# One encoder layer on one core: the first projections split the next block's weights during this block's products, without GpSimd

## The chip, the core and the metric

The kernel runs on one core of a Trainium2 chip. The core has five engines that each run their own instruction queue in order: TensorE (PE in the rows; its weight loads are PEld), VectorE (DVE), ScalarE (ACT), GpSimd (POOL) and SyncE (SP), which here only issues transfers. An engine waits at an instruction until the instructions or transfers of others that it depends on are done. The metric is the device time of one execution in microseconds (us). Time before: 1261.2 us, the median of three runs (1259.64 to 1262.53).

## The reference

One encoder layer over 512 tokens of width 1024, in float32. Only the head of it matters here: a conditioning vector gives six modulation vectors, the first two of which scale and shift x, and the result u is projected by one wide matrix.

```python
mod = jnp.einsum('bd,dn->bn', silu(c), w_ada) + b_ada           # 1024 -> 6 * 1024
sh_a, sc_a, g_a, sh_f, sc_f, g_f = jnp.split(mod[:, None, :], 6, axis=-1)
u = x * (1.0 + sc_a) + sh_a
proj = jnp.einsum('bsd,dn->bsn', u, w_in)                       # 512 x 1024 by 1024 x 1952
cq, ckv, k_rope, dq, dk, dv = jnp.split(proj, IN_SPLITS, axis=-1)
...                                                             # latent attention and differential attention
s12 = einsum('bqhmd,bkhmd->bmhqk', dqb, dk) * DIFF_SCALE + bias # bias from the relative positions
p12 = softmax(s12);  a = p12[:, 0] - lam * p12[:, 1]
...                                                             # output projection, layer norm
ffn = expert_choice_ffn(u, w_router, w_gate, w_up, w_down)      # 16 experts, 64 tokens each
```

## The kernel before

All large operands stand in 24 pages of the on-chip memory, each 128 partitions by 8 KB; `pages.get` and `pages.put` hand out whole pages or parts of them while the program is built, and a transfer or a write into a reused page waits for its last reader.

**Stage 1** (the loop `for i in range(KB)`, L409 to L455) runs over the eight blocks i of 128 input features. For each block four transfers come in on SP's queue, two blocks ahead (`stage1_load`): two of 512 KB with rows of w_ada (`wadaT`), 256 KB of x transposed (`xt`) and 512 KB of the projection's weights (`wd`, 128 by 1024). Then:

- `mod_finish` on VectorE: two multiply-and-sum passes over 128 by 1024 (L217), each with a read of its accumulator, and two one-column operations (L226, L228) give the block's scale and shift in `modc`.
- ScalarE applies them to `xt` (L416). ScalarE also makes the high part of `xt` and of both halves of `wd` (`hi_of`, L136: a copy rounded to a shorter float), and the low part is the difference to it: of `xt` on VectorE (`split`, L236), of the weights on GpSimd for blocks 1 to 7 and on VectorE for block 0 (L422).
- TensorE multiplies: `mm3` is three products, high by high, high by low, low by high. Four banks take the 512 columns of queries and keys with the weights as the stationary operand, four the 512 columns of values with u as the stationary one: 8 times 3 = 24 products of 128 by 512 a block (L121), 192 in the stage, summed over the blocks in the eight banks. The first product of a block needs the high parts, the second the low part of `xt`, the third the low part of the weights.

In block 0 two small products with `rb` and two copies (L145) prepare the relative-position table, which a transfer `f_d` and a transfer `bias_d<-f_d` (1792 KB) spread out in memory; `bias_steps` (L273, one GpSimd operation) and `bias_table` (L279 to L285) find out whether the positions are consecutive, and a branch on GpSimd skips the general table.

All of this stage's order is written out by hand (`manual_schedule`): each engine runs what stands in the code in that order. The stage ends with `q_split(0)`, `q_split(1)` and `rope_tables`. From `start.close()` on, through both attentions, a planner of the framework sets the order on each engine, from its own estimate of when each operation could start; it is free to move products of the remaining projection columns (`q_mm`, 24 products for each of seven column groups) between the score products (`diff_scores`, L521, 16 units of six products) and the softmax passes (`diff_soft`, L536, which read the score banks and the rows of the bias table loaded at L505). From the layer norm on the order is written by hand again, and the program ends with the 16 experts, whose 403 MB of weights come through SP's queue (`prefetch`, L968) as pages come free.

Of the kernel before, what the change touches and what calls it, by code (L numbers as in the profile page):

```python
# [9 lines left out]
F32R = mybir.dt.float32r  # L10
# [3 lines left out]
OP = mybir.AluOpType  # L14
# [87 lines left out]
def encoder_layer(ctx: ExitStack, tc: tile.TileContext, xT, x, wadaT, cvec, colp, rowp, rows, cst, pos, posr,  # L102
# [28 lines left out]
    def ff(ap):  # L131
        return ap.bitcast(F32)

    def hi_of(eng, dst, src, scale=1.0):
        if eng is ACT:
            return ACT.activation(dst, src, AF.Copy, scale=scale)  # L136
        else:
            assert scale == 1.0
            eng.tensor_copy(dst, src)
# [104 lines left out]
    def stage1_load(i):  # L244
        mw = mod_pair(i, i, 8 + i, True)
        hx, xt = pages.get(2, old=OLD1)
        hw, wd = pages.get(4, old=OLD1)
        if i == 0:
            SP.dma_start(wd[:, :512], w_a[i][:, :512])
            SP.dma_start(xt, xT[i])  # L250
            SP.dma_start(wd[:, 512:], w_a[i][:, 512:])
        else:
            SP.dma_start(xt, xT[i])
            EP["s1"] = SP.dma_start(wd, w_a[i])
        if i == 0:
            SP.dma_start(rb, relb)
            SP.dma_start(ohp[:32], bass.AP(tensor=cst.tensor, offset=cst.offset + C_OH, ap=[[C_W, 32], [1, 1024]]))
        st1[i] = (mw, hx, xt, hw, wd)
# [146 lines left out]
    bias_flag()  # L405
    stage1_load(0)
    stage1_load(1)
    for i in range(KB):
        mw, hx, xt, hw, wd = st1[i]  # L409
        if i != 1:  # L410
            mod_finish(mw)
        whh, pg = pages.get(8, F32R)
        wh = HL(pg[:, :1024], pg[:, 1024:])
        if i == 0:
            hi_of(ACT, wh.hi[:, :512], wd[:, :512])
        ACT.activation(xt, xt, AF.Identity, scale=modc[:, 8 + i:9 + i], bias=modc[:, i:i + 1])  # L416
        uh, u = split(xt, 512, DVE)
        for c in (slice(0, 512), slice(512, 1024)):
            eng = POOL if i else DVE
            if i or c.start:  # L420
                EP["hi"] = hi_of(ACT, wh.hi[:, c], wd[:, c])
            eng.tensor_tensor(wh.lo[:, c], wd[:, c], ff(wh.hi[:, c]), op=OP.subtract)  # L422
        U.append(u)
        Uh.append(uh)
        XT.append(xt)
# [1 line left out]
        pages.put(hw)  # L427
        if i + 2 < KB:
            stage1_load(i + 2)
        for n in range(4):  # L430
            mm3(BK[n], wh[:, n * P:(n + 1) * P], u[:, :], i == 0, i == KB - 1)
        if i == 0:
# [1167 lines left out]
```

## Time and profile before

| | |
|---|---|
| median of three runs | 1261.2 us |
| profiled execution: its time, its span | 1258.0 us, 1256.2 us |
| stage 1, first to last of its 192 products | 11.9 to about 69.6 us |
| busy share of the span: TensorE, VectorE, ScalarE, GpSimd | 93%, 30%, 18%, 5% |
| mean transfer rate over the span, and in the experts' part | 363 GB/s, 421 GB/s |

The time line of the profile gives the start of a piece, its length, the engine, line, tiles and the count of instructions that run without a break, and in brackets the idle time before it with what ended it. The table of waits sums these. A table by stretch gives the busy time of each engine in it, with the granted clock of TensorE (1.00 is 2.4 GHz, 0.50 is 1.2 GHz) and the share of the transfer engines. Engines with a q (SPq) are the engine's issuing queue.

### The profile page before, as it was taken

Reading aid. Unit: us, or ns where it says so; the run is one execution under the profiler, and the core shown is the slowest. Engines: PE = TensorE matmul, PEld = TensorE weight load, DVE = VectorE, ACT = ScalarE, POOL = GpSimd, SP = SyncE. Lnnn points to the kernel's source line nnn. Section 1 sums busy time; section 2 is a strip of 40 time slices with the busy share of each in tenths; the row PEclk is TensorE's granted clock in tenths of the full one; section 3 lists DMA queues with packets and bytes.
Section 4 is the critical chain, followed back from the end, with each engine's and each line's share of the span. In section 5 each row is a group of like instructions: output and inputs, shape, how many; then the busy total and the mean of one; then the engine's idle time right before and its main releaser. Section 6 shows DMA issues by size and latency. Waiting matters only on the chain.

```text
span 1256.2 us, 14042 instructions
## 1 busy us (share of the span) xinstructions
PE 1167.8 (93%) x5657; PEld 553.8 (44%) x5657; DVE 374.9 (30%) x813; ACT 229.4 (18%) x473; POOL 57.1 (5%) x45
## 2 busy tenths in 40 slices
PE   8899998998999999999998799789978997999896
PEld 5677676766434433433433243224323432343232
DVE  5779899867101111010110102010101110111016
ACT  3465785443010000000000000000000000001001
POOL 2500000000000320000000000000000000000003
PEclk8999999999999999999999999999999999999999
DMA  9872524497999999999999999999999999999993
GB/s 341 301 244 86 185 98 167 158 365 284 373 421 421 422 418 421 421 421 421 421 421 421 422 420 422 422 422 421 421 421 421 421 422 421 421 422 421 421 401 149
DMA packets 76360, 456.03 MB, mean 363 GB/s; under 512 B 8285, under 2 KB 8669, under 8 KB 28163
## 3 DMA queue, kind: packets, MB, share of 16 engines
q1 hardware_dynamic: 76002, 455.02, 89.3%
q8 instruction: 44, 0.72, 0.2%
q14 instruction: 24, 0.19, 0.0%
q10 hardware_dynamic: 290, 0.10, 0.0%
HBM read 452.98 MB, written 3.95 MB: 364 GB/s over the span
## 4 chain that ended last, share of the span: by engine, by line
PE 38%; DMA 35%; DVE 2%; issue 0%; POOL 0%; ACT 0%; POOLq 0%; SPq 0%; DVEq 0%; ACTq 0%
PE bk L121 21%; PE bk L1338 16%; DMA pg<-in_w_up_dram 16%; DMA pg<-in_w_gate_dram 9%; DMA pg<-in_w_down_dram 9%; PE bk L1369 1%; DVE small L1212 0%; DVE ohg L1214 0%; POOL pg L1467 0%; DVE lst L1449 0%; PE bk L1262 0%; POOLq L1596 0%; PE bk L1287 0%; DVE mv L1450 0%; DVE pg L1406 0%
## 5 line engine op out<-in xcount | busy, mean ns | idle before, releaser
L1338 PE MATMUL bk<-pg,xs 128*64 128x512 f32 x2048 | 474.3, 601 | 50.5 <-DMA pg<-in_w_up_dram 50.5
L121 PE MATMUL bk<-pg,pg 128*64 128x512 f32 (+3 forms) x2138 | 463.9, 479 | 17.4 <-ACT pg L136 6.0
L121 PEld LDWEIGHTS bk<-pg,pg 128*64 128x64 f32 (+1 forms) x2138 | 236.6, 159 | 195.2 <-issue 130.4
L1338 PEld LDWEIGHTS bk<-pg,xs 128*64 128x64 f32 x2048 | 148.2, 137 | 348.0 <-issue 244.3
L1363 DVE TENSOR_TENSOR pg<-pg,bk 128x512 f32<-128x512 f32 x32 | 21.9, 687 | 341.6 <-PE bk L1338 313.2
L143 ACT ACTIVATE pg<-bk 128x512 f32<-128x512 f32 (+1 forms) x97 | 54.8, 582 | 358.3 <-PE bk L1369 321.3
L1273 DVE TENSOR_TENSOR pg<-pg,bk 128x512 f32<-128x512 f32 x56 | 38.5, 687 | 123.1 <-PE bk L121 122.7
L1256 DVE TENSOR_SCALAR xs<-bk,Gc,Bc 128x128 f32<-128x128 f32 x32 | 13.1, 409 | 206.7 <-PE bk L121 206.7
L121 PEld LDWEIGHTS bk<-ohg,pg 128*128 128x128 f32 x512 | 59.7, 192 | 27.3 <-issue 27.3
L121 PE MATMUL bk<-ohg,pg 128*128 128x128 f32 x512 | 66.1, 282 | 0.5 <-DVE ohg L1244 0.5
L121 PE MATMUL bk<-pg,ohg 128*128 128x512 f32 x120 | 59.3, 617 | 0.2 <-DVE pg L1406 0.2
L1254 ACT ACTIVATE xs<-bk,Bc,Gc 128x128 f32<-128x128 f32 x32 | 14.6, 457 | 199.8 <-PE bk L121 199.8
L143 ACT ACTIVATE ohg<-bk 128x512 f32<-128x512 f32 x8 | 4.8, 597 | 238.1 <-PE bk L1262 238.1
L136 ACT ACTIVATE pg<-pg 128x512 fp32r<-128x512 f32 (+2 forms) x63 | 42.7, 709 | 20.1 <-DVE pg L910 4.0
L236 DVE TENSOR_TENSOR pg<-pg,pg 128x512 fp32r<-128x512 f32 (+1 forms) x40 | 37.1, 936 | 16.5 <-ACT pg L136 16.3
L1423 POOL TENSOR_TENSOR pg<-pg,pg 128x512 f32<-128x512 f32 x4 | 5.1, 1277 | 786.5 <-DVE lst L1422 786.5
L1022 DVE CUSTOM_DVE_ANT_0 pg<-pg,pg 128x1024 f32<-128x1024 f32 x32 | 38.8, 1218 | 1.5 <-DMA pg<-in_wadaT_dram 1.5
L121 PEld LDWEIGHTS bk<-pg,ohg 128*128 128x128 f32 x120 | 20.4, 189 | 38.2 <-issue 37.5
L1406 DVE SCALAR_TENSOR_TENSOR pg<-bk,lst,pg 128x512 f32<-128x512 f32 x16 | 12.0, 751 | 74.2 <-PE bk L121 73.4
L1359 ACT ACTIVATE pg<-bk 128x512 f32<-128x512 f32 x32 | 18.8, 598 | 60.2 <-PE bk L1338 60.2
L1369 PEld LDWEIGHTS bk<-csb,pg 128*128 128x128 f32 x128 | 17.7, 207 | 26.9 <-DVE pg L1363 13.9
L217 DVE CUSTOM_DVE_ANT_0 pg<-pg,pg 128x1024 f32<-128x1024 f32 x16 | 24.6, 1571 | 5.8 <-DMA pg<-in_wadaT_dram 5.8
(223 smaller groups left out, 606.7 us busy)
## 6 DMA issues: line engine op xcount, KB each, us to landing
pg<-in_w_gate_dram SPq DMA_DIRECT2D x128, 1024.0 KB, 19.8
pg<-in_w_up_dram SPq DMA_DIRECT2D x128, 1024.0 KB, 19.8
pg<-in_w_down_dram SPq DMA_DIRECT2D x120, 1024.0 KB, 19.8
pg<-in_wadaT_dram SPq DMA_DIRECT2D x16, 1024.0 KB, 5.0
pg<-in_wadaT_dram SPq DMA_DIRECT2D x16, 512.0 KB, 8.0
pg<-in_w_down_dram SPq DMA_DIRECT2D x16, 512.0 KB, 10.9
pg<-bias_d SPq DMA_DIRECT2D x16, 256.0 KB, 3.5
pg<-in_w_out_dram SPq DMA_DIRECT2D x8, 512.0 KB, 3.2
```

Source lines behind the costliest of these rows:

```text
L121: PE.matmul(o, l, r, start=start, stop=stop)
L136: return ACT.activation(dst, src, AF.Copy, scale=scale)
L143: ACT.activation(dst, src, AF.Copy)
L217: DVE.tensor_tensor_reduce(out=w2[:, j], in0=w2[:, j], in1=cs, scale=1.0, scalar=0.0, op0=OP.mult, op1=OP.add, accum_out=modr[:, n:n + 1])
L236: lo_eng.tensor_tensor(lo, src, ff(hi), op=OP.subtract)
L1022: i = DVE.tensor_tensor_reduce(out=w2[:, j], in0=w2[:, j], in1=cs, scale=1.0, scalar=0.0, op0=OP.mult, op1=OP.add, accum_out=modr[:, n:n + 1])
L1254: ACT.activation(xs[:, k, :], src, AF.Identity, scale=Gc[:, k:k + 1], bias=Bc[:, k:k + 1])
L1273: DVE.tensor_add(acc[t][:, c], acc[t][:, c], bank)
L1338: PE.matmul(banks[c][r], xs[:, k, r], w[e][:, c * 512:(c + 1) * 512], start=k == 0, stop=k == 7)
L1359: ACT.activation(EP["HS"][:, c * 512:(c + 1) * 512], banks[c], AF.Silu)
L1363: DVE.tensor_tensor(s, s, U[c], op=OP.mult)
L1369: PE.transpose(G[c % 2][:, i * P:(i + 1) * P], sj[:, i // 2, i % 2, :], ident)
```

## The change

The loop body is reordered. The page of the split weights of block i+1 is taken, both its high parts are made (`w_hi` on ScalarE) and its modulation rows are summed (`mod_finish` on VectorE) in block i's turn, after block i's own splits and before block i's products in the code, for i from 1 to 6; block 1's modulation rows were summed in block 0's turn already. In turn i VectorE makes the two low parts of the weights (`w_lo`, L419) while ScalarE scales and rounds `xt`, and then the low part of `xt` (L443). All low parts are VectorE's; GpSimd keeps `bias_steps`, two memsets, the flag with its branch, and `rope_tables`. No operation is added or left out, and the transfers and their sizes are the same. Lines after the loop stand 27 lower (L521 is L548 then).

```diff
@@ -405,21 +405,43 @@
     bias_flag()
     stage1_load(0)
     stage1_load(1)
+    HALVES = (slice(0, 512), slice(512, 1024))
+    wsp = {}
+
+    def w_page(i):
+        whh, pg = pages.get(8, F32R)
+        wsp[i] = whh, HL(pg[:, :1024], pg[:, 1024:])
+
+    def w_hi(i, c):
+        EP["hi"] = hi_of(ACT, wsp[i][1].hi[:, c], st1[i][4][:, c])
+
+    def w_lo(i, c):
+        DVE.tensor_tensor(wsp[i][1].lo[:, c], st1[i][4][:, c], ff(wsp[i][1].hi[:, c]), op=OP.subtract)
+
+
     for i in range(KB):
         mw, hx, xt, hw, wd = st1[i]
-        if i != 1:
+        if i == 0:
             mod_finish(mw)
-        whh, pg = pages.get(8, F32R)
-        wh = HL(pg[:, :1024], pg[:, 1024:])
+        if i < 2:
+            w_page(i)
         if i == 0:
-            hi_of(ACT, wh.hi[:, :512], wd[:, :512])
+            w_hi(0, HALVES[0])
         ACT.activation(xt, xt, AF.Identity, scale=modc[:, 8 + i:9 + i], bias=modc[:, i:i + 1])
-        uh, u = split(xt, 512, DVE)
-        for c in (slice(0, 512), slice(512, 1024)):
-            eng = POOL if i else DVE
-            if i or c.start:
-                EP["hi"] = hi_of(ACT, wh.hi[:, c], wd[:, c])
-            eng.tensor_tensor(wh.lo[:, c], wd[:, c], ff(wh.hi[:, c]), op=OP.subtract)
+        if i < 2:
+            uh, u = split(xt, 512, DVE)
+            for c in HALVES:
+                if i or c.start:
+                    w_hi(i, c)
+                w_lo(i, c)
+        else:
+            uh, pg = pages.get(4, F32R)
+            u = HL(pg[:, :512], pg[:, 512:])
+            hi_of(ACT, u.hi, xt)
+            for c in HALVES:
+                w_lo(i, c)
+            DVE.tensor_tensor(u.lo, xt, ff(u.hi), op=OP.subtract)
+        whh, wh = wsp.pop(i)
         U.append(u)
         Uh.append(uh)
         XT.append(xt)
@@ -427,6 +449,11 @@
         pages.put(hw)
         if i + 2 < KB:
             stage1_load(i + 2)
+        if 1 <= i < KB - 1:
+            w_page(i + 1)
+            for c in HALVES:
+                w_hi(i + 1, c)
+            mod_finish(st1[i + 1][0])
         for n in range(4):
             mm3(BK[n], wh[:, n * P:(n + 1) * P], u[:, :], i == 0, i == KB - 1)
         if i == 0:
```

On VectorE, from the end of block 2's modulation to block 3's operand, before (pg_25_219 holds the parts of `xt`, pg_20_182 the rows of w_ada for block 3):

```order
L228 TENSOR_TENSOR modc<-modr,cols 128x1
L236 TENSOR_TENSOR pg_25_219<-pg_9_120,pg_25_219 128x512
L217 ISA pg_20_182,modr<-pg_20_182,pg_1_78 128x1024
L217 ISA modr 128x1
L217 ISA pg_20_182,modr<-pg_20_182,pg_1_78 128x1024
L217 ISA modr 128x1
L226 SCALAR_TENSOR_TENSOR modc<-modr,cols 128x1
L228 TENSOR_TENSOR modc<-modr,cols 128x1
L236 TENSOR_TENSOR pg_25_219<-pg_15_139,pg_25_219 128x512
```

and now (pg_22_188 and pg_29_232 hold the parts of the weights of blocks 2 and 3):

```order
L228 TENSOR_TENSOR modc<-modr,cols 128x1
L419 TENSOR_TENSOR pg_22_188<-pg_15_139,pg_22_188 128x512 x2
L443 TENSOR_TENSOR pg_25_221<-pg_9_120,pg_25_221 128x512
L217 ISA pg_20_182,modr<-pg_20_182,pg_1_78 128x1024
L217 ISA modr 128x1
L217 ISA pg_20_182,modr<-pg_20_182,pg_1_78 128x1024
L217 ISA modr 128x1
L226 SCALAR_TENSOR_TENSOR modc<-modr,cols 128x1
L228 TENSOR_TENSOR modc<-modr,cols 128x1
L419 TENSOR_TENSOR pg_29_232<-pg_21_185,pg_29_232 128x512 x2
L443 TENSOR_TENSOR pg_25_221<-pg_15_139,pg_25_221 128x512
```

The two low parts of the weights now stand between the modulation of a block and the low part of its operand; the order of VectorE's other work in the stage is the same, except that block 5's modulation now comes ahead of the four operations of `bias_table`.

On GpSimd, the head of its queue, before and now as one difference (pg_5_106 is the row of positions, pg_21_185 a page for constants):

```order
-L422 TENSOR_TENSOR pg_18_174<-pg_9_120,pg_18_174 128x512 x2
-L422 TENSOR_TENSOR pg_24_217<-pg_15_139,pg_24_217 128x512 x2
 L273 TENSOR_TENSOR pg_5_106<-pg_5_106 1x511
-L422 TENSOR_TENSOR pg_31_261<-pg_21_185,pg_31_261 128x512 x2
-L608 MEMSET pg_21_185 64x512
-L609 MEMSET pg_21_185 64x512
-L422 TENSOR_TENSOR pg_37_303<-pg_28_229,pg_37_303 128x512 x2
```

The fourteen low parts go, and the one operation of `bias_steps`, which stood behind four of them, is now the first on this queue.

On TensorE, in the part that the planner orders, around the scores of the differential attention's units 6 and 7 (bk_73 takes the products of a column group of `q_mm`), before:

```order
L521 MATMUL bk_68<-pg_67_2601 128x512
L521 MATMUL bk_66<-pg_67_2601 128x512
L121 MATMUL bk_72<-pg_65_2593,pg_1_78 128x128 x4
L121 MATMUL bk_73<-pg_12_130,pg_100_2843 128x512 x6
L121 MATMUL bk_73<-pg_25_219,pg_100_2843 128x512 x6
L121 MATMUL bk_73<-pg_38_305,pg_100_2843 128x512 x6
L121 MATMUL bk_73<-pg_53_2482,pg_100_2843 128x512 x6
```

and now:

```order
L548 MATMUL bk_67<-pg_67_2601 128x512
L121 MATMUL bk_73<-pg_12_130,pg_100_2843 128x512 x6
L121 MATMUL bk_73<-pg_25_221,pg_100_2843 128x512 x6
L121 MATMUL bk_73<-pg_38_307,pg_100_2843 128x512 x6
L121 MATMUL bk_73<-pg_53_2484,pg_100_2843 128x512
L582 MATMUL bk_71<-csb,pg_15_139 128x128 x4
L121 MATMUL bk_72<-pg_65_2593,pg_1_78 128x128 x4
L548 MATMUL bk_68<-pg_67_2601 128x512
L548 MATMUL bk_66<-pg_67_2601 128x512
```

Nineteen of this group's 24 products moved from behind unit 7's scores to a place ahead of them. Between the second score unit and the output projection many such pieces changed places; behind that the order on TensorE is the same.

## Rows read from the trace of the kernel before

**Rows 1.** The page's fourth part: the chain that ended last, by engine.

```profile
PE 38%; DMA 35%; DVE 2%; issue 0%; POOL 0%; ACT 0%; POOLq 0%; SPq 0%; DVEq 0%; ACTq 0%
```

**Rows 2.** Time line of TensorE, 10 to 75 us: start, length, count, idle before.

```profile
19.55 13.91 PE L121 MATMUL bk<-pg,pg 128*128 128x512 f32 x60
33.69 0.74 PE L121 MATMUL bk<-pg,pg 128*128 128x512 f32 x2 [0.23 <-ACT pg L136]
35.04 5.25 PE L121 MATMUL bk<-pg,pg 128*128 128x512 f32 x22 [0.62 <-POOL pg L422]
40.59 0.74 PE L121 MATMUL bk<-pg,pg 128*128 128x512 f32 x2 [0.29 <-ACT pg L136]
42.24 5.26 PE L121 MATMUL bk<-pg,pg 128*128 128x512 f32 x22 [0.92 <-POOL pg L422]
48.13 0.73 PE L121 MATMUL bk<-pg,pg 128*128 128x512 f32 x2 [0.63 <-ACT pg L136]
51.96 17.70 PE L121 MATMUL bk<-pg,pg 128*128 128x512 f32 x70 [3.09 <-POOL pg L422]
69.58 0.96 PE L521 MATMUL bk<-pg 64*128 64x512 f32 x6
```

**Rows 3.** Stretches: length, busy time of the five engines, clock, DMA share, GB/s.

```profile
52.00:54.00 2.00, 2.00 (x5) 1.61 (x6) 1.64 (x2) 1.36 (x3) 1.16 (x1) 0.50 0.26 104
110.00:120.00 10.00, 8.32 (x38) 6.53 (x35) 10.00 (x29) 6.13 (x16) 0.00 (x0) 0.83 0.17 53
380.00:400.00 20.00, 19.98 (x102) 8.43 (x100) 5.04 (x8) 1.65 (x3) 0.00 (x0) 1.00 1.01 420
```

**Rows 4.** Time line of GpSimd, 20 to 62 us.

```profile
26.02 3.52 POOL L422 TENSOR_TENSOR pg<-pg,pg 128x512 fp32r<-128x512 f32 x2 [5.15 <-ACT pg L136]
29.50 2.01 POOL L273 TENSOR_TENSOR pg<-pg 1x511 int32<-1x511 int32 x1
50.64 2.52 POOL L422 TENSOR_TENSOR pg<-pg,pg 128x512 fp32r<-128x512 f32 x2 [7.03 <-DVE modc L226]
```

**Rows 5.** Time line of VectorE, 8 to 56 us.

```profile
12.47 1.29 DVE L422 TENSOR_TENSOR pg<-pg,pg 128x512 fp32r<-128x512 f32 x2
20.36 1.05 DVE L236 TENSOR_TENSOR pg<-pg,pg 128x512 fp32r<-128x512 f32 x1
21.34 1.21 DVE L217 CUSTOM_DVE_ANT_0 pg<-pg,pg 128x1024 f32<-128x1024 f32 x1
25.45 0.69 DVE L236 TENSOR_TENSOR pg<-pg,pg 128x512 fp32r<-128x512 f32 x1 [1.55 <-ACT pg L136]
26.06 2.33 DVE L217 CUSTOM_DVE_ANT_0 pg<-pg,pg 128x1024 f32<-128x1024 f32 x1
30.55 0.98 DVE L226 SCALAR_TENSOR_TENSOR modc<-modr,cols 128x1 f32<-128x1 f32 x1
40.65 0.41 DVE L279 CAST pg<-pg 1x511 f32<-1x511 int32 x1
43.28 1.42 DVE L217 CUSTOM_DVE_ANT_0 pg<-pg,pg 128x1024 f32<-128x1024 f32 x1
```

**Rows 6.** ScalarE in the time line of the first 75 us.

```profile
23.93 0.82 ACT L416 ACTIVATE pg<-pg,modc 128x512 f32<-128x512 f32 x1 [5.14 <-DVE modc L228]
```

**Rows 7.** SyncE's queue, 0 to 75 us; the middle row gives median landing.

```profile
34.48 0.33 SPq L254 DMA_DIRECT2D pg<-in_w_a_dram  x1
pg<-in_w_a_dram SPq DMA_DIRECT2D x7, 512.0 KB, 7.7
66.30 3.14 SPq L505 DMA_DIRECT2D pg<-bias_d  x5
```

**Rows 8.** Line L505's own view: issue to landing of its 16 loads.

```profile
DMA to landing us min/median/max: 2.6/3.5/8.2
```

**Rows 9.** First softmax pass, VectorE, in the time line of 64 to 90 us.

```profile
77.54 0.68 DVE L536 CUSTOM_DVE_ANT_0 pg<-bk,pg 128x512 f32<-128x512 f32 x1
```

**Rows 10.** TensorE's later time line: a score unit's wait.

```profile
112.03 0.96 PE L521 MATMUL bk<-pg 64*128 64x512 f32 x6 [1.68 <-DVE st L536]
```

## Prediction

> **What bounds the kernel now.** I read the chain that ended last first. It belongs to TensorE and to the transfers, 38% and 35% of the span; no other engine has over 2% [rows 1]. The experts' part, from about 320 us on, runs with the transfer engines full (share 1.01, 420 GB/s) and TensorE busy 19.98 of 20 us [rows 3]. The change touches nothing there, so it counts only by how much earlier that part starts. Ahead of it, it is TensorE's idle time that can be gained, so I read TensorE's time line of the first 75 us next, then what GpSimd, VectorE and ScalarE do at its gaps.
>
> Stage 1 starts well: 60 products run from 19.55 us without a break, to 33.46 (half of block 0, blocks 1 and 2). Then each block starts late and breaks once: two products, a gap, 22 products. The gaps are 0.23, 0.62, 0.29, 0.92, 0.63 and 3.09 us, and the three that stand inside a block were ended by GpSimd's L422, the low part of the weights [rows 2]. That is what the reader is to see: the third product needs GpSimd. After the longest gap the granted clock is 0.50 for a while, that is 1.2 GHz instead of 2.4 [rows 3].
>
> Why is GpSimd late? It needs 2.5 to 3.5 us for a block's two low parts, where VectorE made those of block 0 in 1.29 [rows 4, 5]. Ahead of block 5's it stood idle for 7.03 us [rows 4]; that follows its flag and its branch, for the four flag operations began at 40.65 and VectorE was through with them at 43.28 [rows 5]. And it holds up VectorE: the multiply-and-sum pass takes 1.21 us alone and 2.33 beside GpSimd [rows 5], and ScalarE waits 5.14 us for the modulation [rows 6].
>
> **What the change removes.** From 19.55 us to the first score product at 69.58 us TensorE runs 180 products (half a block and seven whole ones) in 50.03 us [rows 2]. At the rate of the unbroken stretch, 13.91 us for 60, they need 41.73. The difference, 8.3 us, is gaps, ends of broken pieces and the slow clock after the longest gap. All of it goes if VectorE and ScalarE keep ahead of TensorE.
>
> **Does VectorE keep ahead?** It takes over seven blocks' low parts of weights, 7 times 1.29 = 9.0 us [rows 5]. One block's round is now, without GpSimd beside it: from the first multiply-and-sum pass to ScalarE's scaling 23.93 - 21.34 = 2.59 us, from there to the low part of `xt` 25.45 - 23.93 = 1.52 us [rows 5, 6], with the two low parts (1.29) done inside that time, and 0.69 for the low part of `xt` [rows 5]: 4.80 us. TensorE needs 24 products of 13.91/60, that is 5.56 us a block [rows 2]. So VectorE wins 0.76 us a block. Its starting point: in block 1 it begins the low part of `xt` at 20.36, needs 0.69 and 1.29, and starts block 2's pass at about 22.35 instead of 21.34; block 2's operand is then ready at 22.35 + 4.80 = 27.15, when TensorE, at 19.55 plus 36 products (8.35), needs it at 27.9. It holds. The one extra load is the flag: the four operations of `bias_table` took 43.28 - 40.65 = 2.63 us [rows 5], partly beside GpSimd, which delays block 5's low parts once. Four rounds from 27.15 would give 46.35 and TensorE is free for block 6 at 27.9 + 4 x 5.56 = 50.1; for block 5, three rounds, 41.55 + 2.63 = 44.2 at most against 44.6. Cost 0, with up to 0.5 us for the range. This cover is thin there; without it each us of VectorE is a us of TensorE.
>
> ScalarE does the same operations. It now rounds the next weights before it scales the next `xt`; those rounds wait for transfers, so a late transfer would hold the scaling too. The last block's weights were issued at 34.48 us and such a transfer lands 7.7 us later in the median [rows 7], so they stand by about 42, while block 7 is due at 19.55 + 156 products, 55.7. Cost 0. SyncE's loads keep their order in the stage.
>
> **What it moves to a worse place.** `bias_steps` (L273) now heads GpSimd's queue and runs as soon as the positions land, near 11 us, beside VectorE's first low parts, on which TensorE's block 0 waits. It took 2.01 us beside VectorE and held a one-column operation for 0.98 us [rows 4, 5]. Bounds 0 and 1.0 us; where it falls depends on a landing that I cannot place, so I take 0.5.
> The Trainium skill ("SBUF — State Buffer", "Who interferes with whom") says that a VectorE instruction with two inputs in SBUF contends with a GpSimd instruction that reads SBUF, and that whoever is first holds the shared pair for the whole instruction while the other fully blocks. The 2.33 against 1.21 us agree. By that rule alone VectorE could lose all 2.01 us, and the sum below would be 6.3 us instead of 7.8; the 0.98 us row is what this trace shows, so the sum goes by it.
>
> **What comes late next.** The first softmax pass needs a bias row, and the load of those waits for the table's write: issue at 66.30 [rows 7], landing 2.6 to 8.2 us later [rows 8], 68.9 to 74.5. The table's write is issued behind the stage's transfers, so it does not come earlier. Before, the pass ran at 77.54 [rows 9]; 8 us earlier is 69.5. Units follow TensorE's own filling (about 13 us of column products between the first two units), so a late row stalls VectorE, not yet TensorE. I take 0, and up to 5 us as the other end.
>
> The attentions' order is the planner's and has changed. There single waits of 1 to 2 us stand on TensorE, such as 1.68 us for the softmax pass of a score unit, in a stretch whose clock fell to 0.83 [rows 3, 10]. In the new order 19 products (4.4 us) lie ahead of that very unit, so this wait may go; others may come. Bounds: two such waits less (-3.4 us) or two more (+3.4). I take 0, since rows do not favour a sign.
>
> **The sum.** 8.3 - 0.5 = 7.8 us. The profiled execution took 1258.0 us, 3.2 below the median of 1261.2; with the same saving the changed kernel has 1250.2 in such an execution and **1253.4 us** as a median.
>
> **Rivals.**
> *The bias rows pin the attention.* If they land at the end of their range (74.5), the first pass comes 5 us later than 69.5, and if TensorE's filling runs out before VectorE has caught up, these 5 us are given back: 7.8 - 5.0 = 2.8 us gained, 1258.4 us. For it: the write is untouched. Against: 13 us of products without need of VectorE lie between the units.
> *VectorE becomes the bound of stage 1.* If its passes stayed at 2.33 us without GpSimd beside them, a round would be 4.80 + 2 x 1.12 = 7.0 us, and five blocks would take 1.5 us each more than TensorE: 7.2 us given back, 1260.6, no measurable change. Against: the passes at 21.34 took 1.21 [rows 5].
> *The change doesn't do what it says*: the blocks wait for transfers anyway. Excluded nearly by the issue at 34.48; it would give 1261. I put it with the last.
> *Slower: the planner's new order stalls score units.* TensorE takes its instructions in order; a score unit that is placed too early waits for VectorE to read its bank, with everything behind it, and VectorE is full there (10.00 of 10 us [rows 3]). Fifteen units follow the first. At 0.52 us more on each the 7.8 us are gone; at 0.7 us it is 10.5, 1263.9 us. For it: one unit does wait 1.68. Against: that unit now has products ahead of it.
>
> **How the numbers follow.** The forecast, with its own bounds (-0.5 and -0.5 for the flag and L273, 3.4 to both sides for the order), 1249.5 to 1257.8: 0.70. Bias rows: 0.15. VectorE or the transfers as the bound: 0.06. The stalled units: 0.09, of which 0.02 end within the bound. A median of this kernel tells about 0.2% (2.5 us) from no change, so faster means below 1258.7. Faster 0.70 + 0.15 = 0.85 and same 0.06 + 0.02 = 0.08; slower 0.07. For 8 in 10 the range takes in the forecast's own and most of the bias case: 1249.5 to 1259.0.
>
> **What would show it.** Right: TensorE's products from about 19.5 to 61 us in one piece, the first score product near 61.5, no wait for GpSimd, clock 1.00 throughout 50 to 60, all multiply-and-sum passes near 1.2 us, experts starting some 8 us earlier. Wrong: gaps before blocks ended by L443 or L419 (VectorE bound), by w_a transfers (transfers bound), a first score unit early but L536 of the first units waiting for bias rows, or the gain shown at 70 us and lost in score waits by 230 us.

## The result and the profile after

The changed kernel takes 1251.57 us (median of four runs, 1248.68 to 1253.39) against 1260.42 for the kernel before beside it: a ratio of 0.9933, 95% interval [0.9911, 0.9955]. Timed again on another chip (run 1 below) the ratio was 0.9921 [0.9894, 0.9948]. The profiled execution took 1253.39 us, its span is 1251.6 us.

TensorE's time line of the changed kernel, 10 to 75 us (columns as in [rows 2], which it answers):

```profile
12.88 5.93 PE L121 MATMUL bk<-pg,pg 128*128 128x512 f32 x12 [3.71 <-ACT pg L136]
20.55 41.12 PE L121 MATMUL bk<-pg,pg 128*128 128x512 f32 x180
61.59 0.97 PE L548 MATMUL bk<-pg 64*128 64x512 f32 x6
```

All gaps of [rows 2] are gone: 180 products in one piece of 41.12 us, first score product 7.99 us earlier. What hides the work is seen on VectorE, where a block's round now is 27.90 to 32.62 us, 4.72 us, with every multiply-and-sum pass at 1.22 or 1.23 (2.33 beside GpSimd in [rows 5]), and 0.34 us of waiting for ScalarE left in each round but block 5's. The flag's four operations, before block 5's low parts, run from 39.84 to 41.6:

```profile
10.26 0.99 DVE L226 SCALAR_TENSOR_TENSOR modc<-modr,cols 128x1 f32<-128x1 f32 x1
16.96 0.15 DVE L226 SCALAR_TENSOR_TENSOR modc<-modr,cols 128x1 f32<-128x1 f32 x1
...
27.29 0.69 DVE L443 TENSOR_TENSOR pg<-pg,pg 128x512 fp32r<-128x512 f32 x1 [0.34 <-ACT pg L136]
27.90 1.22 DVE L217 CUSTOM_DVE_ANT_0 pg<-pg,pg 128x1024 f32<-128x1024 f32 x1
...
32.62 1.22 DVE L217 CUSTOM_DVE_ANT_0 pg<-pg,pg 128x1024 f32<-128x1024 f32 x1
...
39.84 0.41 DVE L279 CAST pg<-pg 1x511 f32<-1x511 int32 x1
```

The first row is block 0's and shows the one loss that the change brings in the stage. GpSimd's time line has one operation left there (before, its low parts of the weights filled it, [rows 4]), and the 128x1 operation that runs beside it takes 0.99 us instead of 0.15:

```profile
10.20 1.03 POOL L273 TENSOR_TENSOR pg<-pg 1x511 int32<-1x511 int32 x1 [9.76 <-DMA pg<-in_posr_dram]
```

The start of the attention did not follow by 8 us. ScalarE and VectorE, 60 to 80 us:

```profile
67.81 1.06 ACT L136 ACTIVATE pg<-pg 128x1024 fp32r<-128x1024 f32 x1 [5.45 <-DMA pg<-in_w_q_dram]
68.91 1.23 DVE L236 TENSOR_TENSOR pg<-pg,pg 128x1024 fp32r<-128x1024 f32 x1 [5.37 <-ACT pg L136]
74.82 0.69 DVE L563 CUSTOM_DVE_ANT_0 pg<-bk,pg 128x512 f32<-128x512 f32 x1 [1.36 <-DMA pg<-bias_d]
```

SyncE's queue shows the table's write and the loads of its rows, which answer [rows 7]:

```profile
43.60 0.79 SPq L481 DMA_DIRECT2D bias_d<-f_d  x1
47.14 7.40 SPq L326 DMA_DIRECT2D pg<-in_w_q_dram  x1
...
66.58 4.15 SPq L532 DMA_DIRECT2D pg<-bias_d  x6
```

The first softmax pass comes 13.2 us after the first score product, before 8.0 [rows 2, 9]. And yet the experts' gather (24 products, before first, then after) starts 7.82 us earlier:

```profile
317.37 2.92 PE L121 MATMUL bk<-ohg,pg 128*128 128x128 f32 x24 [0.50 <-DVE ohg L1244]
```

```profile
309.55 2.92 PE L121 MATMUL bk<-ohg,pg 128*128 128x128 f32 x24 [0.50 <-DVE ohg L1271]
```

The two spans differ by 4.6 us only, since the part behind the gather took 3.2 us longer here. The page's row of rates has one slice of 390 GB/s among 420 to 422 there, and 31 us at 390 instead of 421 are 2.3 us of it.

Stretches of the changed kernel, with the columns of [rows 3], which they answer, and the chain by engine, which answers [rows 1]: behind the table's write the transfer engines are a quarter busy, the experts' part is as it was, and the transfers now have more of the chain than TensorE.

```profile
48.00:52.00 4.00, 4.00 (x20) 3.30 (x19) 3.84 (x9) 1.77 (x3) 0.00 (x0) 1.00 0.26 105
380.00:400.00 20.00, 20.00 (x106) 8.74 (x102) 0.82 (x2) 1.51 (x3) 0.00 (x0) 1.00 1.01 421
```

```profile
DMA 43%; PE 31%; DVE 1%; issue 0%; POOL 0%; ACT 0%; POOLq 0%; SPq 0%; DVEq 0%; ACTq 0%
```

The longest single wait of TensorE in the attention stands in its later time line; it answers [rows 10], whose unit no longer waits:

```profile
106.75 6.20 PE L121 MATMUL bk<-pg,pg 128*128 128x512 f32 x19 [2.39 <-ACT pg L648]
```

### The profile page after: what moved, and what is told of

It reads as the page before. It is cut to its first block, busy times and chain, and to the rows that moved or that the text cites. A ratio compares the mean times of both kernels' runs of the same rounds, so it can differ in the third digit from the quotient of the medians.

```text
span 1251.6 us, 14038 instructions
## 1 busy us (share of the span) xinstructions
PE 1173.6 (94%) x5657; PEld 554.1 (44%) x5657; DVE 373.0 (30%) x827; ACT 229.6 (18%) x473; POOL 34.0 (3%) x31
## 4 chain that ended last, share of the span: by engine, by line
DMA 43%; PE 31%; DVE 1%; issue 0%; POOL 0%; ACT 0%; POOLq 0%; SPq 0%; DVEq 0%; ACTq 0%
DMA pg<-in_w_up_dram 17%; PE bk L121 17%; DMA pg<-in_w_down_dram 14%; PE bk L1365 13%; DMA pg<-in_w_gate_dram 11%; PE bk L1242 1%; POOL pg L1494 0%; PE bk L1396 0%; DVE lst L1476 0%; PE bk L1289 0%; POOLq L1623 0%; PE bk L1314 0%; DVE mv L1477 0%; DVE pg L1433 0%; ACT aff L879 0%
## 5 line engine op out<-in xcount | busy, mean ns | idle before, releaser
L1049 DVE CUSTOM_DVE_ANT_0 pg<-pg,pg 128x1024 f32<-128x1024 f32 x32 | 38.7, 1219 | 3.1 <-DMA pg<-in_wadaT_dram 3.1
L236 DVE TENSOR_TENSOR pg<-pg,pg 128x512 fp32r<-128x512 f32 (+1 forms) x34 | 31.0, 920 | 11.5 <-ACT pg L136 11.4
L1433 DVE SCALAR_TENSOR_TENSOR pg<-bk,lst,pg 128x512 f32<-128x512 f32 x16 | 12.0, 751 | 74.5 <-PE bk L121 73.7
L567 ACT ACTIVATE pg<-pg,st 128x512 f32<-128x512 f32 x32 | 23.0, 720 | 11.8 <-DVE st L563 11.6
```

Of the source, the lines that this page charges most:

```text
L236: lo_eng.tensor_tensor(lo, src, ff(hi), op=OP.subtract)
L567: ACT.activation(pm, pm, AF.Exp, scale=-1.0, bias=nm[:, m:m + 1], accum_out=ss[:, m:m + 1])
L1049: i = DVE.tensor_tensor_reduce(out=w2[:, j], in0=w2[:, j], in1=cs, scale=1.0, scalar=0.0, op0=OP.mult, op1=OP.add, accum_out=modr[:, n:n + 1])
```

## The experiments

Two moments divide the 1250 us of every run: the first score product (the end of stage 1) and the gather (the start of the experts' part). Between them lie the attentions and the router. Both are read from TensorE's time line of one profiled execution, and the first softmax pass ("first pass") from VectorE's. "Order" says how many of TensorE's 3463 products, as built, stand outside the longest sequence that a kernel has in common with the changed kernel; "same" means that none does. The executions scatter: the changed kernel's own two (second and third row) differ by 2.2 us at the gather.

| kernel | median us | ratio to before | first score | first pass after it | gather | score to gather | order |
|---|---|---|---|---|---|---|---|
| before | 1260.42 | 1 | 69.58 | 8.0 | 317.37 | 247.8 | 279 elsewhere |
| changed | 1251.57 | 0.9933 [0.9911, 0.9955] | 61.59 | 13.2 | 309.55 | 248.0 | |
| 1 changed, again | 1249.68 | 0.9921 [0.9894, 0.9948] | 60.57 | 14.0 | 307.33 | 246.8 | same |
| 2 GpSimd a block ahead | 1257.89 | 0.9988 [0.9970, 1.0006] | 73.52 | 7.9 | 317.87 | 244.4 | same |
| 3 VectorE, not ahead | 1265.34 | 1.0044 [1.0025, 1.0064] | 64.95 | 8.4 | 322.35 | 257.4 | 401 elsewhere |
| 4 difference on VectorE | 1250.64 | 0.9929 [0.9903, 0.9956] | 59.90 | 14.1 | 307.61 | 247.7 | same |
| 5 GpSimd works beside | 1255.05 | 0.9974 [0.9965, 0.9984] | 67.57 | 11.1 | 313.57 | 246.0 | same |
| 6 table early | 1256.07 | 0.9978 [0.9969, 0.9987] | 73.06 | 1.6 | 314.47 | 241.4 | 413 elsewhere |
| 7 modulation in its turn | 1252.17 (one execution) | | 60.12 | 15.1 | 307.82 | 247.7 | 14 elsewhere |
| 8 before, block 5 on VectorE | 1252.91 (one execution) | | 67.53 | 8.2 | 310.70 | 243.2 | 13 elsewhere |
| 9 table in halves, second late | 1265.83 | 1.0064 [1.0051, 1.0078] | 60.02 | 13.7 | 323.00 | 263.0 | 222 elsewhere |
| 10 table in halves | 1268.42 | 1.0080 [1.0064, 1.0095] | 60.01 | 30.5 | 324.84 | 264.8 | same |
| 11 as 8, timed | 1252.56 | 0.9963 [0.9950, 0.9976] | 67.76 | 8.2 | 310.49 | 242.7 | 13 elsewhere |
| 12 table over 16 engines | 1246.80 | 0.9922 [0.9908, 0.9935] | 60.72 | 7.9 | 303.57 | 242.9 | 1 elsewhere |

Runs 1 to 4 shared one chip, 5 to 8 a second, 9 to 11 a third, 12 a fourth; ratios are to the kernel before on the same chip.

### Run 1: the changed kernel again

> The changed kernel again, as the yardstick for the runs beside it on this chip. Both theories below expect its stage 1 as in its first trace: the 180 products of stage 1 in one piece of 41.1 us, the first score product near 61.6 us, and a time 7 to 9 us under the kernel before.

In the stage it did: 41.09 us in one piece. The first score product came at 60.57 us and the time lies 10 us under the kernel before beside it, both 1 us better than expected. Its first products began at 12.90 us, as in the first trace (12.88), but the first twelve took 4.91 us instead of 5.93: the granted clock of 14 to 20 us was 0.80 here and 0.61 there. So one microsecond of the first score product's place is the execution's.

### Run 2: GpSimd, one block ahead

```diff
-        DVE.tensor_tensor(wsp[i][1].lo[:, c], st1[i][4][:, c], ff(wsp[i][1].hi[:, c]), op=OP.subtract)
+        (POOL if i else DVE).tensor_tensor(wsp[i][1].lo[:, c], st1[i][4][:, c], ff(wsp[i][1].hi[:, c]), op=OP.subtract)
```

> The changed kernel with the low parts of the weights of blocks 1 to 7 given back to GpSimd; order, pages and transfers stay as in the changed kernel, so GpSimd works one block ahead. Theory A (GpSimd itself was the trouble, because it slows VectorE's passes and is slow itself): multiply-and-sum passes beside it take 2.3 us and GpSimd's two low parts 2.5 to 3.5 us, VectorE's round comes to some 6 to 7 us against TensorE's 5.56, breaks of about 1 us a block return, and 5 to 8 us of the gain are lost: first score product at 66 to 70 us. Theory B (what was missing was only the lead of one block): TensorE runs on without a break except behind the flag's branch, and at most 2 us are lost: first score product by 63.5 us.

Theory A, and worse than it said. TensorE, and GpSimd's two low parts of block 5:

```profile
34.46 0.50 PE L121 MATMUL bk<-pg,pg 128*128 128x512 f32 x1 [0.66 <-ACT pg L136]
54.89 18.70 PE L121 MATMUL bk<-pg,pg 128*128 128x512 f32 x70 [6.88 <-POOL pg L419]
```

```profile
52.95 3.13 POOL L419 TENSOR_TENSOR pg<-pg,pg 128x512 fp32r<-128x512 f32 x2 [13.29 <-remote]
```

Blocks 2 to 4 each wait 0.6 to 0.9 us for VectorE's chain (its round was 27.53 to 34.44, 6.9 us), and none of them for GpSimd: the block of lead works. But block 5's low parts stand behind the flag and GpSimd's branch. VectorE had the flag at 46.1 us, GpSimd's next operation began at 52.95, 6.9 us later, and the lead of one block does not cover that. So run 2 loses 13 us to run 1 by two causes: the slower rounds, and one gap of 6.88 us behind the branch.

### Run 3: VectorE, no block ahead

```diff
-            eng = POOL if i else DVE
+            eng = DVE
```

> The kernel before with the low parts of the weights of blocks 1 to 7 on VectorE instead of GpSimd, and nothing else: the code order of the kernel before, so each low part of the weights stands behind the low part of the block's operand. Theory A (GpSimd was the trouble): VectorE's round is 4.80 us plus the two low parts that no longer stand inside its wait for ScalarE, 1.29, that is 6.1 us against TensorE's 5.56; about 0.5 us a block is lost from block 3 on, 2 to 3 us in all, and the first score product comes at 63 to 65 us, 4 to 6 us gained on the kernel before. Theory B (the lead is what counts): each block again breaks once after its second product, 4 us or more stay lost, first score product at 66 us or later.

In stage 1 theory A: rounds of 5.93 us (26.48 to 32.41), one break of 1.45 us behind the flag, ended at 46.46, with a granted clock of 0.50 from 48 to 50 us, first score product at 64.95, 4.6 us gained. The kernel is slower all the same. TensorE, then ScalarE:

```profile
74.23 6.12 PE L121 MATMUL bk<-pg,pg 128*128 128x512 f32 x17 [8.32 <-ACT pg L143]
```

```profile
69.66 1.06 ACT L136 ACTIVATE pg<-pg 128x1024 fp32r<-128x1024 f32 x1 [7.41 <-DMA pg<-in_w_q_dram]
```

The planner put the rounding of the next w_q block ahead of ScalarE's copies out of TensorE's banks. The w_q transfer was late, ScalarE waited 7.41 us for it, and TensorE 8.32 us for the banks. A second wait of the same kind follows at 112.12 us (3.97 us on TensorE, while ScalarE waited 4.14 us for a w_q load). This is the slower rival in another shape: two long waits instead of fifteen short ones.

### Run 4: the difference of the positions on VectorE

```diff
-        POOL.tensor_tensor(irow[:, 512:1023], irow[:, 1:512], irow[:, 0:511], op=OP.subtract)
+        DVE.tensor_tensor(irow[:, 512:1023], irow[:, 1:512], irow[:, 0:511], op=OP.subtract)
...
             mod_finish(st1[1][0])
+            bias_steps()
...
-        if i == 2:
-            bias_steps()
```

> The changed kernel with the difference of the positions (the one operation of bias_steps) moved from the head of GpSimd's queue to VectorE, behind the second modulation, where VectorE waits 2.5 us for ScalarE. If the operation on GpSimd blocks VectorE's one-column operation, as the first trace reads (0.99 us where it takes 0.15), that operation is back at 0.15 us, TensorE's stage starts 0.7 to 1.0 us earlier, and the first score product comes at 60.6 to 60.9 us; the time is 0.7 to 1.0 us less, which is less than the medians can tell. If the 0.99 us has another cause (the landing of a transfer), nothing moves.

VectorE's time line, the two operations in question:

```profile
9.86 0.15 DVE L226 SCALAR_TENSOR_TENSOR modc<-modr,cols 128x1 f32<-128x1 f32 x1
16.08 0.67 DVE L273 TENSOR_TENSOR pg<-pg 1x511 int32<-1x511 int32 x1
```

It was GpSimd: 0.15 us again. TensorE's 180 products begin at 18.87 instead of run 1's 19.55, at nearly the same granted clock from 14 to 20 us (0.81 and 0.80), and the score product is 0.67 us earlier. The gather is not (307.61 against 307.33), nor the time.

```profile
18.87 41.09 PE L121 MATMUL bk<-pg,pg 128*128 128x512 f32 x180
```

### Run 5: GpSimd's work beside, its results unused

```diff
+        if i:
+            for c in HALVES:
+                POOL.tensor_tensor(xs0.rearrange("p k s -> p (k s)")[:, c], wd[:, c], ff(wh.hi[:, c]), op=OP.subtract)
```

> The changed kernel, and beside it GpSimd makes the fourteen subtractions of the kernel before once more, of the same operands, into a scratch tile that nobody reads: work is added, none is left out. Theory A (GpSimd's work slows VectorE just by running beside it): multiply-and-sum passes go from 1.22 to about 2.3 us, VectorE's round from 4.73 to some 7 us against TensorE's 5.56, gaps of 1 to 1.5 us a block that VectorE or ScalarE ends (never GpSimd), and the first score product comes at 65 to 68 us. Theory B (only the waiting for GpSimd's results cost time before): passes stay at 1.22, TensorE runs the 180 products in 41.1 us, first score product near 61.

Theory A. TensorE's first gap, and on VectorE a pass beside GpSimd and one without it:

```profile
30.08 0.50 PE L121 MATMUL bk<-pg,pg 128*128 128x512 f32 x1 [2.27 <-ACT pg L136]
```

```profile
25.24 2.30 DVE L217 CUSTOM_DVE_ANT_0 pg<-pg,pg 128x1024 f32<-128x1024 f32 x1
30.67 1.22 DVE L217 CUSTOM_DVE_ANT_0 pg<-pg,pg 128x1024 f32<-128x1024 f32 x1
```

Rounds of 6.84 us (30.06 to 36.90), no wait of TensorE for GpSimd in the stage, and the score product 7.0 us later than in run 1. Merely by running, GpSimd's subtractions cost most of what the change had gained in the stage, though only those of blocks 1 to 4 ran beside the passes; the last six came from 59.42 us on, behind the flag's branch. They held a page that a w_q load waited for (12.6 us on SyncE's queue), so the first pass, 11.1 us behind the score, is not the change's.

### Run 6: the table's write two blocks earlier

```diff
+        if i == 3:
+            SP.dma_start(bass.AP(tensor=bias_d.tensor, offset=bias_d.offset, ap=[[P * 1024, 4], [1024, P], [1, 896]]),
+                         bass.AP(tensor=f_d.tensor, offset=f_d.offset + 127, ap=[[1024, 4], [-1, P], [1, 896]]))
...
-            SP.dma_start(bass.AP(tensor=bias_d.tensor, offset=bias_d.offset, ap=[[P * 1024, 4], [1024, P], [1, 896]]),
-                         bass.AP(tensor=f_d.tensor, offset=f_d.offset + 127, ap=[[1024, 4], [-1, P], [1, 896]]))
```

> The kernel with the difference on VectorE, and the write of the relative-position table is issued in block 3's turn instead of block 5's, some 9 us earlier. In the changed kernel the first softmax pass runs 14.0 us after the first score product, in the kernel before 8.0, and in the run with GpSimd a block ahead, which has the same order of TensorE's products, 7.9; there the attention part is 3.6 us shorter. Theory A (the write of the table and the load of w_q beside it hold the start of the attention, and some of the 8 us are given back there): the first pass comes at 67 to 69 us and the experts' gather 2 to 4 us earlier than in the kernel with the difference alone, so about 1247 us. Theory B (TensorE's filling covers the late rows fully): the first pass comes earlier, the gather does not, and the time stays near 1250. Against both: the write then runs beside the weights of blocks 6 and 7, and the planner's order of the attention changes, which can move the gather by some us either way.

Neither: the write held up block 6's operands. Beside it the transfer rate fell to 109 GB/s, SyncE's next issue took 11.57 us, and TensorE stood for 10.33:

```profile
28.87 11.57 SPq L207 DMA_DIRECT2D pg<-in_wadaT_dram  x1
```

```profile
34.00:38.00 4.00, 4.00 (x19) 3.31 (x18) 3.66 (x6) 2.36 (x4) 0.00 (x0) 1.00 0.27 109
```

```profile
59.61 13.52 PE L121 MATMUL bk<-pg,pg 128*128 128x512 f32 x48 [10.33 <-ACT pg L136]
```

From the first score product on, with the table there, it took 241.4 us, some 6 less than the changed kernel, but in another order: it pointed at the write without settling it.

### Run 7: the modulation in its own turn

```diff
-        if i == 0:
+        if i != 1:
             mod_finish(mw)
...
-            mod_finish(st1[i + 1][0])
```

> The changed kernel with the modulation of a block summed in the block's own turn again; the high parts of the weights stay a block ahead on ScalarE, the low parts stay inside VectorE's wait for ScalarE. VectorE's queue then reads the same but for bias_table, which comes ahead of block 5's modulation. If the lead that counts is the queue's order and not the turn in the code, stage 1 is as in the changed kernel: 180 products in 41.1 us, first score product near 61. If the turn counts, TensorE breaks before each block.

180 products in 41.09 us, score product at 60.12: the turn in which the code stands counts for nothing here, the queue's order does. Summing the modulation rows "a block ahead" was no part of the gain. What is left of the change is that the low parts of the weights stand inside VectorE's wait for ScalarE, for which their high parts have to be made before.

### Runs 8 and 11: the kernel before, block 5's low parts alone on VectorE

```diff
-            eng = POOL if i else DVE
+            eng = POOL if i and i != 5 else DVE
```

> The kernel before with the low parts of block 5's weights alone on VectorE; GpSimd keeps the other six blocks. Block 5 is the one whose low parts stood behind GpSimd's flag branch. If the branch alone made the longest gap (3.09 us and the slow clock after it), that gap goes, the smaller ones stay or grow by 1 us for block 6, and the first score product comes at 65 to 67 us instead of 69.6. If GpSimd is late anyway, the gap moves to block 6 and less than 1 us is gained.

> The kernel before with block 5's low parts on VectorE, timed. If its one profile is typical (gather at 310.7 us against 317.4 before, though stage 1 ended only 2.1 us earlier), it takes 1252 to 1254 us, 6 to 7 us under the kernel before. If that execution was a lucky one, 1256 to 1258.

The longest gap goes: blocks 4 and 5 meet without one (26 products in a piece), the small ones stay, and the score product comes 1.8 to 2.1 us earlier, less than the 65 to 67 us expected. TensorE in run 11:

```profile
48.30 6.71 PE L121 MATMUL bk<-pg,pg 128*128 128x512 f32 x26 [0.61 <-ACT pg L136]
55.63 5.28 PE L121 MATMUL bk<-pg,pg 128*128 128x512 f32 x22 [0.63 <-POOL pg L422]
```

But the gather comes 6.9 us earlier. The other 5 us were won in the attention, which the edit does not touch: 242.7 us instead of 247.8, in an order that differs from the changed kernel's in 13 products and from the kernel before's in 291. So the better order is not the change's own: moving two subtractions brought it as well.

### Runs 9 and 10: the table in two halves

```diff
+    def table_write(g):
+        d = SP.dma_start(bass.AP(tensor=bias_d[g].tensor, offset=bias_d[g].offset, ap=[[P * 1024, 2], [1024, P], [1, 896]]),
+                         bass.AP(tensor=f_d.tensor, offset=f_d.offset + g * 2048 + 127, ap=[[1024, 2], [-1, P], [1, 896]]))
...
                 fs.append(lambda b=b: q_load(b + 2))
+                if b == 2:
+                    fs.append(lambda: table_write(1))
```

Run 10 has `b == 0` there, so that the second half follows the first w_q load at once. The rows of `bias_d` are divided between two tensors accordingly.

> The kernel with the difference on VectorE, and the relative-position table is written in two halves: the two heads that are read first at the old place, the other two only behind a later load of w_q. In the four runs with TensorE's order of the changed kernel whose stage 1 ended at 60 to 62 us, the part from the first score product to the experts' gather took 246.8 to 248.0 us, with the table and the w_q beside it landing near 66 us; in the two whose stage ended at 67.5 and 73.5 us with the same or nearly the same order, 243.2 and 244.4. Theory A (some 4 us of the stage's gain are given back to that one write): with half of it in the way the w_q load and the first rows land 6 to 10 us earlier, the first softmax pass comes at 67 to 70 us instead of 74, that part takes 243 to 244 us, and the time is some 1246 us. Theory B (the 4 us lie elsewhere): the first pass comes earlier, but the part still takes 247 us, and the time stays near 1250. The planner's order of the attention changes with the edit (2500 of 3475 products stand elsewhere), so a difference of the two of up to 5 us could be its own; the waits on TensorE between 70 and 110 us must tell.

> As the run before, but the second half of the table is written right behind the first w_q load of the attention, ahead of the next. Theory A: that w_q lands early as well, the next one some 6 us late; first pass at 67 to 71 us, time 1246 to 1249. Theory B: time near 1250. If it and the run before differ by more than 3 us, the order of the attention decides and neither is settled.

Both theories failed on their common ground, that half a table takes half the time. (Their count of moved products was wrong too: 222 of 3463 stand elsewhere in run 9, and none in run 10, which has the changed kernel's order.) The bias rows were issued at 65.53 us in run 9 as before, and while a half was under way the transfer engines were busy to 0.13 at 53 GB/s (run 9, then run 10):

```profile
48.00:52.00 4.00, 4.00 (x20) 3.30 (x18) 3.41 (x8) 2.86 (x4) 0.00 (x0) 1.00 0.13 53
```

```profile
56.00:60.00 4.00, 4.00 (x18) 3.03 (x17) 3.00 (x7) 3.17 (x5) 0.00 (x0) 1.00 0.13 53
```

Half the bytes at half the rate. So the second half was a second write of some 20 us (run 10: issued at 52.32, the share at 0.13 until about 70), and TensorE waited 12.73 us (run 9, for a bank that ScalarE could not empty while it waited 15.31 for w_q) and 15.89 us (run 10, for the first bias rows):

```profile
104.93 2.07 PE L121 MATMUL bk<-pg,pg 128*128 128x128 f32 x8 [12.73 <-ACT pg L599]
```

```profile
91.30 1.65 PE L554 MATMUL bk<-pg 64*128 64x512 f32 x6 [15.89 <-DVE st L569]
```

The share goes with the outer dimension of the transfer: 4 heads, 0.26; 2 heads, 0.13; that is 4 and 2 engines of 16. The Trainium skill ("DMA: Bandwidth & Descriptors", "Why a DMA increments its semaphore by 16 and not by 1") says that a transfer runs on the largest number of engines, up to 16, that divides the outermost dimension (longer than 1) of both sides; these rows agree, and run 12 follows from it.

### Run 12: the table's write over 16 engines

```diff
-    f_d = dram.tile([4, 1024], F32, name="f_d")
+    f_d = dram.tile([16, 928], F32, name="f_d")
...
-            SP.dma_start(f_d, ohp[32:36, :])
+            fo = ohp[32:36, 96:1024]
+            SP.dma_start(bass.AP(tensor=f_d.tensor, offset=f_d.offset, ap=[[4 * 928, 4], [928, 4], [1, 928]]),
+                         bass.AP(tensor=fo.tensor, offset=fo.offset, ap=[list(fo.ap[0]), [-32, 4], [1, 928]]))
...
-            SP.dma_start(bass.AP(tensor=bias_d.tensor, offset=bias_d.offset, ap=[[P * 1024, 4], [1024, P], [1, 896]]),
-                         bass.AP(tensor=f_d.tensor, offset=f_d.offset + 127, ap=[[1024, 4], [-1, P], [1, 896]]))
+            SP.dma_start(bass.AP(tensor=bias_d.tensor, offset=bias_d.offset, ap=[[32 * 1024, 16], [1024, 32], [1, 896]]),
+                         bass.AP(tensor=f_d.tensor, offset=f_d.offset + 31, ap=[[928, 16], [-1, 32], [1, 896]]))
```

> The kernel with the difference on VectorE, and the table is written from a source of 16 rows (each head's row four times, shifted by 32) instead of 4, in one transfer of the same size at the same place; the order of TensorE's products is that kernel's, but for one product that moves by four places. The two runs before showed that half the table takes as long as the whole, at half the share of the transfer engines (0.13 instead of 0.26): the outer dimension of the transfer seems to set how many of the 16 engines work on it. If so, the share is near 1.0 and the write takes some 6 us instead of 22; the w_q load behind it and the bias rows land by 55 us. Theory A (about 4 us of the gain are given back to the late table and w_q): the first softmax pass then comes 8 us or less after the first score product (at 67 to 68 us instead of 74), the part from there to the experts' gather takes 243 to 244 us instead of 247.7, and the time is 1246 to 1247. Theory B (the 4 us belong to something else in the attention): the pass comes earlier, the part still takes 247 to 248 us, and the time stays near 1250. If the write still takes over 15 us, the theory on the outer dimension is wrong and nothing moves.

Theory A. The stretch after the issue, the first softmax pass, and TensorE's longest wait in the differential attention (2.39 us in the changed kernel, 1.62 here):

```profile
46.00:50.00 4.00, 4.00 (x20) 3.30 (x19) 3.67 (x9) 1.80 (x4) 0.00 (x0) 1.00 1.03 409
```

```profile
68.63 0.68 DVE L564 CUSTOM_DVE_ANT_0 pg<-bk,pg 128x512 f32<-128x512 f32 x1
```

```profile
103.11 4.61 PE L121 MATMUL bk<-pg,pg 128*128 128x512 f32 x19 [1.62 <-ACT pg L649]
303.57 2.92 PE L121 MATMUL bk<-ohg,pg 128*128 128x128 f32 x24 [0.50 <-DVE ohg L1272]
```

No wait for the table or for that w_q is left, and in an order that differs from run 4's by the one moved product the part from score to gather is 242.9 us instead of 247.7. The gather is 4.0 us earlier than in run 4, the span 4.5 us shorter (1243.1, 1247.6). In the timed ratios the two overlap (0.9922 and 0.9929, on two chips), so the 4 us stand on one profiled execution of each. Its median, 1246.8 us, is the lowest here, but the ratio does not tell it from the changed kernel (0.9921 in run 1).

Where the late table costs its time shows product by product, since runs 4 and 12 have the same order but for one product. Run 4 is 2.3 us behind after the first 92 products from the score on, where it has waits of 0.71, 0.19 and 0.89 us for VectorE that run 12 has not. It is 4.5 us behind after its longest wait, for a bank that ScalarE has to empty, and the 19 products that follow: the wait is 0.8 us longer (2.39 against 1.62), and the products take 6.05 us instead of 4.61, with the granted clock at 0.50 from 106 to 108 us. Run 4, then run 2, whose table came in time:

```profile
105.36 6.05 PE L121 MATMUL bk<-pg,pg 128*128 128x512 f32 x19 [2.39 <-ACT pg L647]
```

```profile
116.46 4.59 PE L121 MATMUL bk<-pg,pg 128*128 128x512 f32 x19 [2.24 <-ACT pg L648]
```

The wait itself stands there with the table in time too, and in run 1 it was as long as in run 4 (2.40 us) without the slow clock behind it (4.61 us for the 19 products). So 1.4 of the 4.5 us are the clock's and do not come in every execution.

## Why the prediction was right, point by point

**The stage's 8.3 us: right.** From the first of the 180 products to the score the time fell from 50.03 to 41.04 us, 9.0 us; the stage began 1.0 us later, and 8.0 us are left at the score. 41.12 us of products against the 41.73 worked out, VectorE's round 4.72 against 4.80, the flag 1.7 us against at most 2.63, no gap. Its reason was right too, in two halves that the runs separate. Without GpSimd beside it VectorE keeps up (run 5: GpSimd's bare presence costs 7.0 us, the rival "VectorE becomes the bound" had priced it at 7.2). And the low parts of the weights fit inside the wait for ScalarE (run 3, without that: 4.6 us of the gain are left). The block of lead for GpSimd would have been worth nothing (run 2). Two readings on the way were wrong, and the sum used neither. The 5.14 us in [rows 6] stand before block 2, whose passes took 1.21 us without GpSimd, so that row does not show GpSimd holding up ScalarE. And the 7.03 us in [rows 4] are not the branch's alone: ScalarE had block 5's high parts ready only at 48.60 us.

**ScalarE and the stage's transfers at 0: right.** One piece of 180 products leaves no room for either.

**`bias_steps` at 0.5 us: 0.7.** Run 4 measures it, inside the bounds of 0 and 1.0. The Trainium skill's rule ("SBUF — State Buffer", "Who interferes with whom") is borne out as to the mechanism, since the 128x1 operation was held to within 0.05 us of GpSimd's end (10.26 + 0.99, 10.20 + 1.03). VectorE lost 0.84 us, what was left of an operation that took 1.03 here; so neither the 0.98 nor the 2.01 of the rows was the right scale by itself.

**The bias rows at 0: wrong, about 4 us.** The rows came where the prediction said (issue at 66.58, first pass at 74.82, just past the late end of its 68.9 to 74.5), but "13 us of products lie between the units" did not cover it. In the changed kernel the loss is made up of small waits at the first units (0.18 and 0.91 us), the wait of 2.39 us for a bank at 106.75, where run 12 has 1.62, and a slow clock behind it (6.20 us for 19 products). In the four executions with this order (to within 14 products) and a late table, score to gather takes 246.8 to 248.0 us (the changed kernel, runs 1, 4, 7), in the four with the table in time 242.7 to 244.4 (runs 2, 8, 11, 12), and run 12 puts the one in place of the other. With rows later still, in the same order, run 10 takes 264.8. The upper bound of 5 us was right, the choice of the lower end wrong. The row that would have told stood in [rows 3]: at 52 to 54 us the share of the transfer engines was 0.26 at 104 GB/s, with w_q queued behind. It was read for the clock alone.

**The planner's order at 0, bounds 3.4: wrong, 3.4 to 5.1 us won.** The old order takes 247.8 us with the table in time (first pass 8.0 us behind the score), the new one 242.7 to 244.4. The wait of 1.68 us at unit 7 [rows 10] went, as the prediction thought possible. It was one of several: between score and gather TensorE idles 15.0 us in the old order and 9.2 and 9.3 in runs 8 and 11, and two more long waits stand in the old one alone, so the "two such waits" of the bounds were too few:

```profile
199.32 2.92 PE L121 MATMUL bk<-pg,pg 128*128 128x512 f32 x11 [1.63 <-ACT pg L136]
205.55 0.66 PE L921 MATMUL bk<-csb,pg 128*128 128x128 f32 x4 [1.94 <-ACT pg L143]
```

So the sum, 7.8 us at the gather against 7.82 measured, is right by two errors of 4 us that cancel, and that is luck; run 1, the same kernel, gives 10.0 at the gather. Without the better order the gain would have been about 4 us, near the rival of the bias rows; with the table in time it would have been 12, and run 12, with the moved operation of run 4 in it, shows 13.8 at the gather. The medians gave 8.9 us for the changed kernel, 10.0 for run 1 and 10.7 for run 12, each against the kernel before beside it, so what the traces show of the table is not told apart in the times.

**The slower rival (0.09)** did not come here but came in run 3, with the same mechanism of order by another queue: its price, 9.6 us between score and gather, is near the 10.5 that it gave.

## What to carry to other kernels

When VectorE paces a pipeline, count GpSimd's two-input work beside it as VectorE's own time (here 1.1 us for each pass of 1.2), and put VectorE's spare work where it waits for another engine. Where a planner orders what comes after an edit, compare that part alone, from one landmark to the next: here it moved by 5 to 10 us to either side, as much as the edit itself. Read the share of the transfer engines in every stretch, not only the clock: here a quarter meant that a transfer with an outer dimension of 4 was in the way, and reshaping it brought forward the loads queued behind it.

## What the runs showed that was not expected

- A transfer of 1792 KB from memory to memory with an outer dimension of 4 ran at 105 GB/s and 0.26 of the engines, at most 23 us (issued at 43.60, the rows behind it at 66.58); half of it no faster, at 53 GB/s and 0.13; over 16 rows at 409 GB/s and 1.03 with the others. A w_q load of 512 KB issued 3.5 us behind the slow one was waited for until 67.81, 20.7 us after its issue.
- From VectorE's flag to GpSimd's next operation behind the branch pass 6.9 us (run 2, 46.1 to 52.95), 7.4 us in the kernel before (43.28 to 50.64, [rows 4, 5]) and 10.9 us in run 5 (48.56 to 59.42); how much of it is the branch was not measured apart.
- The same first twelve products took 5.93 us in one execution and 4.91 in another, at granted clocks of 0.61 and 0.80 in 14 to 20 us, with idle times of 3.71 and 3.25 us ahead of them.
